# Splitting the last input projection of a forgetting-attention layer into a query half and a gate half, with the last four heads in one list of steps

## The chip, the cores and the metric

The kernel runs on one core of one Trainium2 chip. The metric is device time in microseconds (us) of one execution, from start to end, and the time of a kernel is the median of its runs. Engines are called by their names: TensorE (PE) for matrix products, with its weight load (PEld); VectorE (DVE) and ScalarE (ACT) for elementwise work; GpSimd (POOL); SyncE (SP), which here issues nearly all DMA transfers.

## The reference

Two layers over 512 tokens of width 2048. The first is differential attention; then keys, values and forget-gate logits are projected once (`shared_kv`); the second layer is forgetting attention, which the change touches:

```
def forgetting_attention(h, w_q, w_out, k, v, F):
    proj = h @ w_q
    q, g = jnp.split(proj, 2, axis=-1)
    q = q.reshape(B, S, B_HEADS, B_HEAD_DIM) * (B_HEAD_DIM ** -0.5)
    ...
        decay = jnp.moveaxis(Fq, 1, 2)[..., None] - Fk[:, :, None, :]
        sc = jnp.einsum('bqhd,bkhd->bhqk', qb, k).astype(f32) + decay
        sc = jnp.where(causal, sc, NEG)
        p = jax.nn.softmax(sc, axis=-1)
        return jnp.einsum('bhqk,bkhd->bqhd', p.astype(v.dtype), v)
    ...
    o = o.reshape(B, S, B_WIDTH) * jax.nn.silu(g)
    return o @ w_out
```

It has 16 heads of width 128. `q` is the left half of the projection's 4096 columns and the gate `g` the right half. The result goes through a residual sum and a layer norm.

## The kernel before, in words

**Numbers.** Every matrix operand is split into a high and a low part of a faster 32-bit format; a product is three matmuls (`products`, L172 to L176): high by high, high by low, low by high. A split is a copy on ScalarE and a subtraction on VectorE (`split`, L168 to L170). Tokens lie 128 to a block (4 blocks), the width in 16 row blocks of 128 (`KT`). `Hh[kt]`, `Hl[kt]` hold the transposed input of the running projection, 128 by 512; their 32 buffers turn in a ring (`new_h`).

**Weights.** All projections read one stream of weight tiles (`WeightStream`, L51). A `Job` names the columns, and one tile of it is two row blocks by 512 columns. SyncE loads a tile up to three ahead into four buffers (`wst`), ScalarE and VectorE split it two ahead into three buffers (`whi`, `wlo`, L94 and L95).

**Groups and ticks.** `group` (L303) runs a job: for each of 8 tiles, for each of 4 PSUM banks (`acc`), a burst of 6 matmuls. After each of the 32 bursts `tick` takes one piece from the list `pieces` and issues it, so the attention of an earlier pair of heads is laid between the bursts of a projection. `drain` issues all that is left. The program lists instructions in this order; when the kernel is built, a planner fixes each engine's order, and may put ready products ahead of ones that it expects to wait.

**The input projection of the second layer.** Eight jobs `bj[p]`, one for each pair of heads: 256 columns of queries and 256 of gates side by side. Banks 0 and 1 end as the queries of the two heads (`qh`, `ql`, L1201 and L1202), banks 2 and 3 as their gates (`sgb`, L1207 and L1208). While `bj[p]` runs, the pieces are the attention of pair p - 1 (`attention_pair`, L1303): 26 steps of `attention_b` (L1232). For each head and each of the four token blocks i:

- `score(i)`: products of queries and keys into one of two `sc` banks, then bias, sum and minimum, exponential, reciprocal and scaling (L1244 to L1255), on VectorE but for the exponential;
- `turn(i)`: a 32 by 32 transpose on VectorE (L1264) and a store to DRAM (L1266);
- `send(i)`: four DMAs from there into `pTl` (L1274);
- `take(i)`: the split of the transposed probabilities into `pTh` and `pTl` (L1280, L1281).

`values(0, 2)` and `values(2, 4)` then make the 12 matmuls of the head's output (bank `o`) and multiply by the gate into `ogB` (L1297). There is one `pTh` and one `pTl` for all heads. `load_pair` fetches a pair's values and decay rows, `split_pair` splits its values and keys (`vbh`, `kbh`); both are issued ahead of the last tile of the pair's own job.

**The end.** The outputs `ogB` of 16 heads, split by `split_ogb` (L1313) into new `Hh`, `Hl`, are the input of the output projection. While `bj[7]` runs, heads 0 to 13 are split, two after each tile from the second on. Queries of pair 7 are there only at the end of `bj[7]`, so its attention is laid between the bursts of the first output projection, with the split of heads 14 and 15 as the 27th step; row blocks 14 and 15 are read by the last of the 8 tiles. `out_projection` (L934) runs four jobs of 512 columns. Their residual work (`residual_b`, L1348) adds pieces `scaled` for each token block (`nr`, L1359 and L1360): for the first job into steps of `pieces` that are empty, from the third on, else at the end of the list. At the end of the first job it drains the list ahead of its first evacuation (`ztmp`, L961), and the attention's memory is given to the output.

Of the kernel before, what the change touches and what calls it, by code (L numbers as in the profile page):

```python
# [10 lines left out]
F32 = mybir.dt.float32  # L11
F32R = mybir.dt.float32r
# [4 lines left out]
P = 128  # L17
D = 2048
KT = D // P
# [15 lines left out]
class Job:  # L35


    def __init__(self, src, parts):
        self.src = src
        self.parts = parts  # L40
        self.width = sum(n for _, n in parts)

    def load(self, nc, dst, kt):
        rows = self.src[kt * P : (kt + 2) * P, :]
        off = 0
        for c, n in self.parts:
            nc.sync.dma_start(dst[:, :, off : off + n], rows[:, c : c + n].rearrange("(k p) n -> p k n", p=P))
            off += n


class WeightStream:  # L51
# [15 lines left out]
        self.order.append((job, sub))  # L67

    def add_job(self, job):
        for s in range(KT // 2):  # L70
            self.add(job, s)

    def load(self, upto):
# [37 lines left out]
def tile_yoco(  # L111
# [44 lines left out]
    def acc_bank(name="acc"):  # L156
        return ps.tile([P, 512], F32, name=name, tag="acc", bufs=4)
# [10 lines left out]
    def split(hi, lo, src):  # L168
        S.copy(hi, src)
        V.tensor_tensor(lo, src, hi.bitcast(F32), op=ALU.subtract)  # L170
# [96 lines left out]
    phases = [(0, 0, 4), (1, 0, 8), (0, 4, 12), (1, 8, 16), (0, 12, 16)]  # L267
    kj = [Job(kv_w, [(512 * g, 512)]) for g in range(4)]
    vj = [Job(kv_w, [(2048 + 512 * g, 512)]) for g in range(4)]
    bj = [Job(b_w_in, [(256 * p, 256), (2048 + 256 * p, 256)]) for p in range(8)]  # L270
    oA = [(f, Job(a_w_out, [(512 * f, 512)]), (0, 1, 2, 3)) for f in range(4)]
    oB = [(f, Job(b_w_out, [(512 * f, 512)]), (0, 1, 2, 3)) for f in range(4)]
    for u, k0, k1 in phases:
# [4 lines left out]
    for h in range(2, A_HEADS):  # L278
        ws.add_job(qk[h])
        ws.add_job(vg[h])  # L280
    for j in [o[1] for o in oA] + vj + kj + bj + [o[1] for o in oB]:
        ws.add_job(j)

    pieces = []
# [18 lines left out]
    def group(job, natural, evac, banks=range(4), bg=0, before_sub=None, after_sub=None, hold=0, after_held=None):  # L303


        acc = {b: acc_bank() for b in banks}
        w = job.width
        count = 0
        ns = KT // 2

        def burst(s, b, hi, lo):
            nonlocal count
            for kk in range(2):
                kt = 2 * s + kk
                bs = slice(b * P, (b + 1) * P)
                start, stop = kt == 0, kt == KT - 1
                if natural:
                    products(acc[b][:, :w], (Hh[kt][:, bs], Hl[kt][:, bs]), (hi[kk][:, :w], lo[kk][:, :w]), start, stop)
                else:
                    products(acc[b], (hi[kk][:, bs], lo[kk][:, bs]), (Hh[kt], Hl[kt]), start, stop)  # L320
            if s == ns - 1:
                evac(b, acc[b])
            tick(bg(count) if callable(bg) else bg)
            count += 1

        for s in range(ns - hold):
            if before_sub:
                before_sub(s)
            hi, lo = ws.get(job, s)
            for b in banks:  # L330
                burst(s, b, hi, lo)
            if after_sub:
                after_sub(s)
        for s in range(ns - hold + 3, ns):
            ws.advance(ws.where[(id(job), s)])

            pool, tag = (kpool, "K") if s < ns - hold + 5 else (hpool, "H")
            ws.step(lambda: pool.tile([P, 512], F32R, name="held", tag=tag))
            ws.load(ws.done + ws.STAGES - 1)
        held = [ws.get(job, s, 0) for s in range(ns - hold, ns)]  # L340
        for b in banks if hold else ():
            for k, (hi, lo) in enumerate(held):
                burst(ns - hold + k, b, hi, lo)
                if after_held:
                    after_held(b, k)
                if b == banks[-1] and k < 3:
                    ws.advance(ws.where[(id(job), ns - 1)] + 1 + min(k + 1, 3))


    def cols(name):  # L350
# [536 lines left out]
    for h in range(3, A_HEADS):  # L887
# [34 lines left out]
    def row_bcast(t, src):  # L922
        nc.sync.dma_start(t, src.partition_broadcast(P))
# [271 lines left out]
    def evac_b(p):  # L1195
        def fn(b, acc):
            hd = 2 * p + b % 2
            if b < 2:
                hi = bp.tile([P, T], F32R, name="qh", tag="qh", bufs=2)
                lo = bp.tile([P, T], F32R, name="ql", tag="ql", bufs=2)  # L1200
                S.activation(hi, acc, AF.Copy, scale=QS)  # L1201
# [10 lines left out]
    def load_pair(p):  # L1212
        v = bp.tile([P, TB, 256], F32, name="vld", tag="vld", bufs=1)
        nc.sync.dma_start(v, v_dram[:, 256 * p : 256 * (p + 1)].rearrange("(j p) e -> p j e", p=P))
        cur[p, "vld"] = v
        for hd in (2 * p, 2 * p + 1):
            nf = bp.tile([P, T], F32, name="nfb", tag="nfb", bufs=2)
            row_bcast(nf, f_dram[hd, :])
            cur[hd, "nf"] = nf

    def split_pair(p):
# [3 lines left out]
        cur[p, "vB"] = (vh, vl)  # L1225
        for hd in (2 * p, 2 * p + 1):
            kh = bp.tile([P, T], F32R, name="kbh", tag="kbh", bufs=2)
            kl = bp.tile([P, T], F32R, name="kbl", tag="kbl", bufs=2)
            split(kh, kl, KTs[hd])
            cur[hd, "kB"] = (kh, kl)  # L1230

    def attention_b(hd):  # L1232
        st = {}
# [79 lines left out]
    def split_ogb(hds):  # L1313
        for hd in hds:
            new_h(hd)
            split(Hh[hd], Hl[hd], ogB[hd])

    load_pair(0)
    for p in range(8):
# [110 lines left out]
```

## Time and profile before

| what | value |
|---|---|
| median of 3 runs | 1983.98 us (1981.49 to 1984.32) |
| span of the profiled execution | 1978.1 us |
| TensorE busy | 1936.2 us (98%), 8869 matmuls |
| VectorE busy | 1348.1 us (68%) |
| ScalarE busy | 704.0 us (36%) |
| mean granted clock of TensorE | 0.993 |
| mean DMA rate | 188 GB/s |

The profiled execution is given by its span, from its first to its last instruction; the time of a run also holds what lies around the span. A profile row names the line of the kernel, the engine, the operation and the tiles as `out<-in`. Times in rows are counted from the start of the span. "Idle before" is the time for which the engine stood still ahead of an instruction, with what released it. The granted clock is the share of full speed at which TensorE was allowed to run.

### The profile page before, as it was taken

What the parts mean: (1) busy time and instruction counts of PE and PEld (TensorE: products, weight loads), DVE (VectorE), ACT (ScalarE), POOL (GpSimd) and SP (SyncE); (2) the same over time, 40 slices, a digit from 0 to 9 for tenths busy, and PEclk for the clock granted to TensorE, in tenths of its full rate; (3) what the DMA queues carried; (4) which work ended last, traced back from release to release, by engine and by line L of the source; (5) the groups of instructions that cost most, each with busy time, mean ns of one, the idle gap of its engine ahead of it and who ended that gap; (6) DMA issues with size and microseconds to landing.
All of it is one profiled execution on the core that took longest, in us unless ns stands there. A gap on an engine that the chain in (4) does not pass through costs nothing.

```text
span 1978.1 us, 25283 instructions
## 1 busy us (share of the span) xinstructions
PE 1936.2 (98%) x8869; PEld 1600.8 (81%) x8869; DVE 1348.1 (68%) x2488; ACT 704.0 (36%) x1217; POOL 2.2 (0%) x10
## 2 busy tenths in 40 slices
PE   5999999999999999999999999999999999999997
PEld 4888888888887888788888888888888888887886
DVE  7885678777777778853575665666566666676657
ACT  2422445333332324431264222224343434453123
POOL 0000000000000000000000000000000000000000
PEclk8999999999999999999999999999999999999999
DMA  9993445676776777652345766664355555565522
GB/s 341 356 315 101 135 149 161 211 229 213 228 219 216 221 224 228 204 168 96 117 149 203 251 229 194 227 218 136 112 154 148 155 151 154 153 185 165 199 89 106
DMA packets 319515, 371.40 MB, mean 188 GB/s; under 512 B 57590, under 2 KB 221196, under 8 KB 318620
## 3 DMA queue, kind: packets, MB, share of 16 engines
q1 hardware_dynamic: 317008, 365.57, 58.2%
q10 hardware_dynamic: 2380, 4.21, 0.6%
q8 instruction: 70, 1.15, 0.2%
q14 instruction: 57, 0.47, 0.1%
HBM read 343.27 MB, written 26.43 MB: 187 GB/s over the span
## 4 chain that ended last, share of the span: by engine, by line
PE 87%; DVE 6%; DMA 4%; issue 1%; SPq 1%; ACT 1%; DVEq 0%; ACTq 0%
PE acc L174 25%; PE acc L175 25%; PE acc L176 25%; PE sc L175 2%; PE sc L176 2%; PE sc L174 2%; DMA ms<-in_kv_w_mod_dram 2%; PE o L174 1%; PE o L176 1%; PE o L175 1%; DVE macc L391 1%; DVE wlo L95 1%; DMA sms<-in_w_mod_dram 1%; DMA e<-turned 1%; DMA turned<-e 1%
## 5 line engine op out<-in xcount | busy, mean ns | idle before, releaser
L95 DVE TENSOR_TENSOR wlo<-wst,whi 128x1024 fp32r<-128x1024 f32 (+2 forms) x322 | 384.3, 1195 | 352.3 <-ACT whi L94 349.3
L94 ACT CAST whi<-wst 128x1024 fp32r<-128x1024 f32 (+2 forms) x322 | 331.8, 1031 | 724.9 <-PE acc L176 355.6
L174 PE MATMUL acc<-whi,hh 128*128 128x512 f32 x1232 | 483.3, 395 | 4.1 <-DVE sg L695 2.2
L175 PE MATMUL acc<-wlo,hh 128*128 128x512 f32 x1232 | 482.1, 391 | 0.1
L176 PE MATMUL acc<-whi,hl 128*128 128x512 f32 x1232 | 481.4, 391 | 0.0
L174 PE MATMUL acc<-hh,whi 128*128 128x512 f32 x1184 | 464.2, 392 | 1.7 <-DVE sg L695 1.6
L175 PE MATMUL acc<-hl,whi 128*128 128x512 f32 x1184 | 461.5, 390 | 0.0
L176 PE MATMUL acc<-hh,wlo 128*128 128x512 f32 x1184 | 460.7, 390 | 0.0
L174 PEld LDWEIGHTS acc<-whi,hh 128*128 128x128 f32 x1232 | 232.6, 189 | 51.3 <-issue 2.6
L176 PEld LDWEIGHTS acc<-whi,hl 128*128 128x128 f32 x1232 | 232.2, 188 | 49.1
L175 PEld LDWEIGHTS acc<-wlo,hh 128*128 128x128 f32 x1232 | 232.5, 189 | 46.2 <-DVE wlo L95 0.5
L176 PEld LDWEIGHTS acc<-hh,wlo 128*128 128x128 f32 x1184 | 222.3, 188 | 47.6
L174 PEld LDWEIGHTS acc<-hh,whi 128*128 128x128 f32 x1184 | 222.5, 188 | 46.2 <-issue 2.5
L175 PEld LDWEIGHTS acc<-hl,whi 128*128 128x128 f32 x1184 | 222.6, 188 | 42.0
L391 DVE SCALAR_TENSOR_TENSOR macc<-ms,cact,macc 128x512 f32<-128x512 f32 x300 | 223.7, 746 | 34.2 <-DMA ms<-in_kv_w_mod_dram 17.5
L498 DVE SCALAR_TENSOR_TENSOR sacc<-sms,cact,sacc 128x512 f32<-128x512 f32 (+1 forms) x127 | 89.5, 705 | 5.1 <-DMA sms<-in_w_mod_dram 1.4
L725 ACT ACTIVATE e<-e,mn 128x128 f32<-128x128 f32 (+3 forms) x64 | 36.0, 563 | 111.6 <-DVE mn L721 107.3
L1253 ACT ACTIVATE eb<-eb,mnb 128x128 f32<-128x128 f32 (+1 forms) x64 | 36.0, 563 | 85.9 <-DVE mnb L1250 85.7
L721 DVE CUSTOM_DVE_ANT_0 e<-sc,bias 128x128 f32<-128x128 f32 (+3 forms) x64 | 31.1, 486 | 22.0 <-PE sc L176 21.9
L391 DVE SCALAR_TENSOR_TENSOR macc<-msk,cact,macc 128x512 f32<-128x512 f32 x60 | 45.0, 750 | 1.4
L1250 DVE CUSTOM_DVE_ANT_0 eb<-sc,biasb 128x128 f32<-128x128 f32 (+1 forms) x64 | 31.1, 485 | 19.5 <-PE sc L176 18.8
L822 ACT ACTIVATE ogT<-tr,subg 128x128 f32<-128x128 f32 x64 | 20.0, 364 | 46.0 <-PE tr L820 45.9
(262 smaller groups left out, 1764.5 us busy)
## 6 DMA issues: line engine op xcount, KB each, us to landing
wst<-in_a_w_in_dram SPq DMA_DIRECT2D x240, 256.0 KB, 3.9
ms<-in_w_mod_dram SPq DMA_DIRECT2D x64, 512.0 KB, 4.2
ms<-in_kv_w_mod_dram SPq DMA_DIRECT2D x64, 512.0 KB, 4.3
wst<-in_kv_w_dram SPq DMA_DIRECT2D x64, 512.0 KB, 3.8
wst<-in_b_w_in_dram SPq DMA_DIRECT2D x128, 256.0 KB, 3.0
sms<-in_w_mod_dram SPq DMA_DIRECT2D x56, 512.0 KB, 6.9
wst<-in_a_w_out_dram SPq DMA_DIRECT2D x32, 512.0 KB, 3.7
msk<-in_w_mod_dram SPq DMA_DIRECT2D x64, 256.0 KB, 5.3
```

Source lines behind the costliest of these rows:

```text
L94: self.nc.scalar.copy(hi[:, :, :w], st[:, :, :w])
L95: self.nc.vector.tensor_tensor(lo[:, :, :w], st[:, :, :w], hi[:, :, :w].bitcast(F32), op=ALU.subtract)
L174: PE.matmul(dst, lhs[0], rhs[0], start=start, stop=False)
L175: PE.matmul(dst, lhs[0], rhs[1], start=False, stop=False)
L176: PE.matmul(dst, lhs[1], rhs[0], start=False, stop=stop)
L391: ins = V.scalar_tensor_tensor(acc, w, cact[:, kt : kt + 1], acc, op0=ALU.mult, op1=ALU.add)
L498: V.scalar_tensor_tensor(acc, w, sc, acc, op0=ALU.mult, op1=ALU.add)
L721: V.tensor_tensor_reduce(out=e[:, :w], in0=sc[:, :w], in1=st["bias"][:, (3 - i) * P :], scale=-1.0, scalar=3.0e38, op0=ALU.add, op1=ALU.mi ...
L725: S.activation(e[:, :w], e[:, :w], AF.Exp, bias=mn, scale=-1.0, accum_out=rs)
L822: S.activation(ogT[2 * h + e][:, i * P : (i + 1) * P], pt[:, e * P : (e + 1) * P], AF.Copy, scale=subg[:, e : e + 1])
L1250: V.tensor_tensor_reduce(out=e[:, :w], in0=sc[:, :w], in1=bias[:, :w], scale=-1.0, scalar=3.0e38, op0=ALU.add, op1=ALU.min, accum_out=mn)
L1253: S.activation(e[:, :w], e[:, :w], AF.Exp, bias=mn, scale=-1.0, accum_out=rs)
```

## The change

`bj` keeps seven jobs. The eighth becomes two half jobs: `lastq`, the 256 query columns of heads 14 and 15, and `lastg`, their 256 gate columns. A tile of a half job is four row blocks by 256 columns. `half_group` runs it in two banks with 16 bursts of 6 matmuls. In `lastg` the outputs of heads 0 to 7 are split, one after every second burst. The attention of pairs 6 and 7 becomes one list of 50 steps, `last_pairs`, that starts with `lastq` and runs on into the first output projection; in it heads 14 and 15 follow behind 12 and 13, and the loads and splits of their decay rows, keys and values and the splits of heads 8 to 15 are steps of their own. The lines that laid the attention of pair 7 into the output projection go.

```
+class HalfJob:
+    def __init__(self, src, col):
+        self.src, self.col = src, col
+        self.width = 512
+        self.subs = KT // 4
+    def load(self, nc, dst, kt):
+        rows = self.src[2 * kt * P : (2 * kt + 4) * P, self.col : self.col + 256]
+        nc.sync.dma_start(dst.rearrange("p k (q n) -> p k q n", q=2), rows.rearrange("(k q p) n -> p k q n", q=2, p=P))
...
-    bj = [Job(b_w_in, [(256 * p, 256), (2048 + 256 * p, 256)]) for p in range(8)]
+    bj = [Job(b_w_in, [(256 * p, 256), (2048 + 256 * p, 256)]) for p in range(7)]
+    lastq, lastg = HalfJob(b_w_in, 256 * 7), HalfJob(b_w_in, 2048 + 256 * 7)
...
+    def half_group(job, evac, after_sub):
+        acc = [acc_bank() for _ in range(2)]
+        for s in range(job.subs):
+            hi, lo = ws.get(job, s)
+            for k in range(2):
+                for b in range(2):
+                    for q in range(2):
+                        kt = 4 * s + 2 * k + q
+                        bs = slice(256 * q + b * P, 256 * q + (b + 1) * P)
+                        products(acc[b], (hi[k][:, bs], lo[k][:, bs]), (Hh[kt], Hl[kt]), kt == 0, kt == KT - 1)
+                    if kt == KT - 1:
+                        evac(b, acc[b])
+                    tick(0)
+                after_sub(2 * s + k)
...
+    def last_pairs():
+        sa, ra, da, ta, va = attention_b(12)
+        sb, rb, db, tb, vb = attention_b(13)
+        sc, rc, dc, tc_, vc = attention_b(14)
+        sd, rd, dd, td, vd = attention_b(15)
+        kc, kd = (partial(split_k, hd) for hd in (14, 15))
+        fc, fd = (partial(load_f, hd) for hd in (14, 15))
+        lv, v7 = partial(load_v, 7), partial(split_v, 7)
+        og = [lambda hd=hd: split_ogb((hd,)) for hd in range(B_HEADS)]
+        steps = [
+            [], [sa[0]], [sa[1], lv], [ra[0]], [sa[2], ra[1]], [da[0]], [sa[3], da[1]], [ra[2], fc],
+            [sb[0], ta[0]], [ra[3], da[2]], [sb[1], ta[1]], [rb[0], da[3]], [sb[2], ta[2]], [rb[1]], [sb[3], ta[3]], [rb[2], va[0], fd],
+            [va[1], kc], [db[0], db[1], rb[3]], [db[2], sc[0]], [tb[0], db[3]], [sc[1], tb[1]], [tb[2], kd], [sc[2], tb[3]], [vb[0]],
+            [vb[1], rc[0]], [sc[3], rc[1]], [dc[0], dc[1], v7], [rc[2]], [sd[0]], [tc_[0], rc[3], dc[2]], [tc_[1], dc[3]], [sd[1]],
+            [tc_[2]], [sd[2], tc_[3], og[8]], [rd[0], vc[0]], [vc[1], rd[1]], [sd[3], og[9]], [dd[0], dd[1], rd[2]], [og[10]],
+            [rd[3], dd[2]], [dd[3], og[11]], [td[0]], [td[1], og[12]], [td[2]], [td[3], og[13]], [vd[0]], [vd[1]], [], [og[14]], [og[15]],
+        ]
+        return [todo or None for todo in steps]
...
-        def after(s):
-            if s >= 1:
-                split_ogb((2 * s - 2, 2 * s - 1))
...
-        group(bj[p], False, evac_b(p), before_sub=before, after_sub=after if p == 7 else None)
+        group(bj[p], False, evac_b(p), before_sub=before)
+
+    pieces.extend(last_pairs())
+    half_group(lastq, evac_b(7), lambda s: None)
+    half_group(lastg, lambda b, acc: evac_b(7)(b + 2, acc), lambda s: split_ogb((s,)))
...
-    pieces.extend(attention_pair(7))
-    pieces.append(lambda: split_ogb((14, 15)))
```

Here `s`, `r`, `d`, `t` and `v` with a letter a to d for heads 12 to 15 are `score`, `turn`, `send`, `take` and `values`; `kc`, `kd` split a key, `fc`, `fd` load decay rows, `lv` and `v7` load and split the values of pair 7, and `og` splits a head's output. `load_pair` and `split_pair` are cut into `load_v`, `load_f`, `split_v` and `split_k`, with the same operations.

More of the change, by code (lines that the diff above doesn't have):

```diff
@@ L41, in __init__ @@
         self.width = sum(n for _, n in parts)
+        self.subs = KT // 2
     def load(self, nc, dst, kt):
@@ L69, in add_job @@
     def add_job(self, job):
-        for s in range(KT // 2):
+        for s in range(job.subs):
             self.add(job, s)
@@ L280, in tile_yoco @@
         ws.add_job(vg[h])
-    for j in [o[1] for o in oA] + vj + kj + bj + [o[1] for o in oB]:
+    for j in [o[1] for o in oA] + vj + kj + bj + [lastq, lastg] + [o[1] for o in oB]:
         ws.add_job(j)
@@ L347, in group @@
                     ws.advance(ws.where[(id(job), ns - 1)] + 1 + min(k + 1, 3))
+    def half_group(job, evac, after_sub):
+        acc = [acc_bank() for _ in range(2)]
+        for s in range(job.subs):
+            hi, lo = ws.get(job, s)
[9 more added lines that the diff above has]
+                after_sub(2 * s + k)
     def cols(name):
@@ L1210, in evac_b, with load_v @@
         return fn
-    def load_pair(p):
+    def load_v(p):
         v = bp.tile([P, TB, 256], F32, name="vld", tag="vld", bufs=1)
@@ L1215, in load_pair, with load_f, split_v @@
         cur[p, "vld"] = v
+    def load_f(hd):
+        nf = bp.tile([P, T], F32, name="nfb", tag="nfb", bufs=2)
+        row_bcast(nf, f_dram[hd, :])
+        cur[hd, "nf"] = nf
+    def load_pair(p):
+        load_v(p)
         for hd in (2 * p, 2 * p + 1):
[L1217 to L1221, printed above, removed]
+            load_f(hd)
+    def split_v(p):
         vh = bp.tile([P, TB, 256], F32R, name="vbh", tag="vbh", bufs=1)
@@ L1225, in split_pair, with split_k @@
         cur[p, "vB"] = (vh, vl)
+    def split_k(hd):
+        kh = bp.tile([P, T], F32R, name="kbh", tag="kbh", bufs=2)
+        kl = bp.tile([P, T], F32R, name="kbl", tag="kbl", bufs=2)
+        split(kh, kl, KTs[hd])
+        cur[hd, "kB"] = (kh, kl)
+    def split_pair(p):
+        split_v(p)
         for hd in (2 * p, 2 * p + 1):
[L1227 to L1230, printed above, removed]
+            split_k(hd)
     def attention_b(hd):
@@ L1316, in split_ogb @@
             split(Hh[hd], Hl[hd], ogB[hd])
+    def last_pairs():
[16 more added lines that the diff above has]
+        return [todo or None for todo in steps]
     load_pair(0)
-    for p in range(8):
+    for p in range(7):
         if p:
```

## The prediction

> **What bounds the kernel now.** I read the page first, then the busy time by stage around the place that the change touches, then the waits of TensorE, then the instructions of TensorE and VectorE in order of time.
>
> ```profile
> span 1978.1 us, 25283 instructions
> ...
> PE 1936.2 (98%) x8869; PEld 1600.8 (81%) x8869; DVE 1348.1 (68%) x2488; ACT 704.0 (36%) x1217; POOL 2.2 (0%) x10
> ```
>
> The page says that TensorE is the bound, busy for 1936.2 of 1978.1 us. The change removes no product, so it can only win back idle or slow time of TensorE. Where is that? The stages, in order: the last input projection (job `bj[7]`, which carries the attention of pair 6), the first output projection up to its seventh weight tile, its end, and the start of the second. Columns: length, busy time per engine, granted clock, DMA share.
>
> ```profile
> core 0: us, PE busy (x) PEld busy (x) DVE busy (x) ACT busy (x) POOL busy (x), PEclk, DMA share, GB/s
> 1722.70:1776.90 54.20, 54.20 (x253) 45.26 (x252) 43.39 (x89) 29.78 (x56) 0.00 (x0) 1.00 0.58 172
> ...
> 1776.90:1820.80 43.90, 43.90 (x205) 36.82 (x204) 28.85 (x67) 15.76 (x32) 0.00 (x0) 1.00 0.52 154
> 1820.80:1834.60 13.80, 9.87 (x28) 7.64 (x27) 10.52 (x18) 1.38 (x2) 0.00 (x0) 0.63 0.91 319
> 1834.60:1845.00 10.40, 9.92 (x44) 7.83 (x44) 10.28 (x17) 1.34 (x2) 0.00 (x0) 1.00 0.42 159
> ```
>
> The first two stages are full at full clock. The third is not: 28 matmuls in 13.8 us, and the granted clock fell to 0.63. The waits of TensorE from 1480 us to the end name the causes; there are only three (us in total, times, longest).
>
> ```profile
> PE o L175 <- DVE pTl L1281: 2.5, 1, 2.5
> PE acc L174 <- ACT hh L169: 1.4, 1, 1.4
> PE acc L174 <- DVE ztmp L961: 0.5, 1, 0.5
> ```
>
> TensorE in order of time, start and length first. A busy span has a modelled end, so I count from start to start.
>
> ```profile
> 1804.81 0.40 PE L175 MATMUL o<-pTl,vbh 128*128 128x512 f32 x1
> ...
> 1806.54 0.39 PE L174 MATMUL acc<-whi,hh 128*128 128x512 f32 x1
> ...
> 1820.60 0.39 PE L176 MATMUL acc<-whi,hl 128*128 128x512 f32 x1
> 1820.83 0.40 PE L174 MATMUL o<-pTh,vbh 128*128 128x512 f32 x1
> 1823.72 0.51 PE L175 MATMUL o<-pTl,vbh 128*128 128x512 f32 x1 [2.50 <-DVE pTl L1281]
> ...
> 1826.41 0.41 PE L176 MATMUL o<-pTh,vbl 128*128 128x256 f32 x1
> 1828.25 0.80 PE L174 MATMUL acc<-whi,hh 128*128 128x512 f32 x1 [1.43 <-ACT hh L169]
> ...
> 1834.39 0.41 PE L176 MATMUL acc<-whi,hl 128*128 128x512 f32 x1
> 1834.65 0.39 PE L174 MATMUL acc<-whi,hh 128*128 128x512 f32 x1
> ...
> 1839.45 0.61 PE L174 MATMUL acc<-whi,hh 128*128 128x512 f32 x2
> 1840.54 0.50 PE L174 MATMUL acc<-whi,hh 128*128 128x512 f32 x1 [0.48 <-DVE ztmp L961]
> ```
>
> From 1806.54 to 1820.60 there are 62 steps of a wide product: 0.2268 us each. The last eleven value products of a head took 1806.54 - 1804.81 = 1.73 us at full clock. At 1820.83 TensorE has done all of the first output projection that doesn't need heads 14 and 15, starts the values of head 15 (`o`), and waits for that head's probabilities (`pTl`), then for its gated output as `hh`. What held `pTl` back stands on VectorE and ScalarE:
>
> ```profile
> 1819.32 1.03 ACT L1280 CAST pTh<-pTl 128x384 fp32r<-128x384 f32 x2
> ...
> 1820.59 0.55 DVE L1281 TENSOR_TENSOR pTl<-pTl,pTh 128x384 fp32r<-128x384 f32 x1
> 1821.05 0.68 DVE L1359 SCALAR_TENSOR_TENSOR nr<-nr,g 128x512 f32<-128x512 f32 x1
> ...
> 1822.98 0.68 DVE L1281 TENSOR_TENSOR pTl<-pTl,pTh 128x512 fp32r<-128x512 f32 x1
> ...
> 1828.23 0.69 DVE L170 TENSOR_TENSOR hl<-ogB,hh 128x512 fp32r<-128x512 f32 x1 [0.68 <-ACT hh L169]
> ...
> 1839.80 1.28 DVE L961 TENSOR_TENSOR ztmp<-acc,gate 128x512 f32<-128x512 f32 x2
> ```
>
> ScalarE had its half by 1820.35; VectorE ran residual pieces (`nr`) in between. More such pieces, run by the drain at burst 28, delay the evacuation `ztmp` to 1839.80.
>
> **What the end of attention costs now.** From 1820.60 to 1834.65 are 14.05 us. The wide acc products in it number 16 (one before, 15 from 1828.25 to 1834.39): 16 x 0.2268 = 3.63; the twelve value products 0.23 + 1.73 = 1.96. Work 5.59, loss 8.46 us: the wait of 1823.72 - 1820.83 - 0.23 = 2.66, the gap 1828.25 - 1826.41 - 0.21 = 1.63 (0.21 is a 256-wide step at that clock), and 4.17 that the low clock costs. The second wait: 1840.54 - 1839.45 = 1.09 for two products of 0.45, so 0.64. **Together 9.1 us, all there is to win.**
>
> **Part by part.** *The projection in halves.* Old: 8 weight tiles of two row blocks by 512 columns, 4 banks of 6 products per tile. New: 4 + 4 tiles of four row blocks by 256 columns, 2 banks of 6 products, twice per tile. So 192 products of 0.2268 us on both sides, 24 per tile, and as many weight splits on ScalarE and VectorE: no change. SyncE issues 8 loads of 512 KB in place of 16 of 256 KB, with the same 1 KB rows. Such a load isn't in the trace; the nearest one is
>
> ```profile
> wst<-in_kv_w_dram SPq DMA_DIRECT2D x64, 512.0 KB, 3.8
> ```
>
> The stream loads three tiles ahead, 3 x 24 x 0.2268 = 16.3 us at the least, so a landing of twice 3.8 us is hidden. Bounds: 0 (hidden) and 3.8 (one tile late); I take 0, since no row shows TensorE waiting for a weight load. Fewer issues could only free SyncE, which doesn't set the end; a gain is excluded.
>
> *Queries first.* Their two evacuations now come half a job earlier. In the old order head 14's first score could only follow these at the end of the job:
>
> ```profile
> 1752.88 0.40 PE L174 MATMUL o<-pTh,vbh 128*128 128x512 f32 x1
> ...
> 1771.39 0.40 PE L174 MATMUL o<-pTh,vbh 128*128 128x512 f32 x1
> ...
> 1769.55 0.60 ACT L1201 ACTIVATE qh<-acc 128x512 fp32r<-128x512 f32 x1 [0.76 <-PE acc L176]
> ```
>
> The first two rows are the values of heads 12 and 13, 18.5 us apart. One pair of probability tiles (`pTh`, `pTl`) serves all heads, so heads go through it one after the other, and this is the length of one turn. The values of 14 had to wait until 1804.12, for the scores came after 1769.55.
>
> *The list of steps.* There are 50 steps for 32 bursts of the two half jobs, so 18 are left for the first output projection, the split of head 15 being its 18th. With turns of 18.5 us head 15's values start at 1752.88 + 3 x 18.5 = 1808.4 (the list starts one burst earlier, which I don't count). Then 1.96 for the products and three operations of 0.69 at most: ready by 1812.4. TensorE needs it when all else is done, 1820.83 as now plus the twelve value products that then lie ahead: 1822.8. **Slack 10.4 us.** So 2.66 + 1.63 + 4.17 go. What is late next is nothing in this projection. Four residual pieces fill a free step and the three behind, and the pieces of the second block, drained today at burst 28, get ticks of their own before it; so the 0.64 goes too.
>
> *Queues moved past.* The splits of heads 8 to 13, today in the projection, move behind it: six pairs of casts on ScalarE and VectorE leave the fullest stretch. In their place come scores of 14 and 15. The key and value splits and the loads of decay rows are spread as single steps, each behind the last use of the buffer it takes. SyncE issues in order, and already waits on VectorE:
>
> ```profile
> SPq L1266 <- DVE tb L1264: 20.1, 9, 4.8
> ```
>
> This (us in total, times, longest) is the longest entry between 1720 and 1840 us; sends to the next head and weight loads queue behind it, under 4.8 us at a time, covered by the 16.3 us above.
>
> *VectorE in the gate half.* The price list is from the groups between 1722.7 and 1776.9 us (columns: busy, mean ns):
>
> ```profile
> L95 DVE TENSOR_TENSOR wlo<-wst,whi 128x1024 fp32r<-128x1024 f32 x9 | 11.0, 1221 | 0.9 <-ACT whi L94 0.9
> L170 DVE TENSOR_TENSOR hl<-ogB,hh 128x512 fp32r<-128x512 f32 x13 | 8.8, 674 | 3.6 <-PE acc L175 3.6
> L1244 DVE SCALAR_TENSOR_TENSOR biasb<-nfb,F,mask 128x128 f32<-128x128 f32 (+3 forms) x8 | 4.3, 540 | 0.0
> L1264 DVE STREAM_TRANSPOSE tb<-eb 128x128 f32<-128x128 f32 (+3 forms) x8 | 4.1, 508 | 0.1
> L1281 DVE TENSOR_TENSOR pTl<-pTl,pTh 128x128 fp32r<-128x128 f32 (+3 forms) x8 | 3.9, 482 | 1.3 <-ACT pTh L1280 1.3
> L1250 DVE CUSTOM_DVE_ANT_0 eb<-sc,biasb 128x128 f32<-128x128 f32 (+3 forms) x8 | 3.8, 477 | 0.9 <-PE sc L176 0.8
> L1255 DVE TENSOR_SCALAR eb<-eb,rsb 128x128 f32<-128x128 f32 (+3 forms) x8 | 3.1, 383 | 0.1
> ```
>
> Steps 16 to 31 hold six scores (0.540 + 0.477 + 0.383 = 1.40 each: 8.4), five transposes (2.5), six takes (2.9), eight head splits (5.4), four weight splits (4.9), and some nine other operations (two evacuations of queries, two gated outputs, two key splits, one value split of 1.2, two reciprocals) at about 0.65: 5.9. Sum 30. TensorE's work there is 96 x 0.2268 = 21.8, one and a half heads of values 2.9, and for the 18 products of the scores an estimated 18 x 0.157 = 2.8 (1.73 / 11, the mean step of the value products): 27.5 us. Consecutive VectorE operations overlap (the take at 1820.59 lasts 0.55, the next starts after 0.46), which takes about a tenth off: 27 against 27.5. VectorE is just full there, so it may run a few us late; the weight splits are taken two tiles ahead (48 x 0.2268 = 10.9 us), and the lag is worked off in the output projection. I allow 0.2 us per head in four heads where a value product catches VectorE late: **0.8 us**, between 0 and, each, the 2.66 above; the nearer end is 0, because at full load about 1753 us no wait is listed.
>
> **Sum.** 1978.1 - 9.1 + 0.8 = 1969.8 us of span. The median of 1983.98 is 5.9 us more than the profiled span; with the same around it, **1975.7 us**, 0.42% less. A measurement of this kernel can tell about 0.2%, 4 us, from no change.
>
> **Rivals.** *One stall comes back.* The order of instructions on each engine is fixed when the kernel is built; if VectorE runs late against it at one `o`, TensorE waits once as at 1820.83 and drops its clock again: 2.66 + 4.17 = 6.8 of the 9.1 given back, 1981.7 us. For it: VectorE just full over 27 us. Against: it was nearly full in the first half of `bj[7]` too, and no wait is listed there:
>
> ```profile
> 1722.70:1749.00 26.30, 26.30 (x124) 22.05 (x123) 24.77 (x61) 15.30 (x33) 0.00 (x0) 1.00 0.56 168
> ```
>
> VectorE was busy for 24.77 of 26.30 us there. The clock's part is read from the stage with 0.63, after an idle span of 2.50 us, while the one of 0.48 left it at 1.00.
>
> [...]
>
> *It doesn't do what it says.* Head 15 still comes last, because the one probability tile and SyncE's order stretch each of three turns by (10.4 + 2.7) / 3 = 4.4 us; the wait then stands where it is: 1984.
>
> *Slower.* VectorE decides: the scores and transposes of a head (4 x 1.40 + 4 x 0.508 = 7.6 us) don't fit beside the turn of the head before but lengthen it. This decides from 5.9 us a turn, where head 15 is 7.3 us late. With two turns lengthened by 7.6 and eight more head splits (5.4) in the way it is (15.2 + 5.4) - 10.4 = 10.2 us late; with the gap and the clock (1.63 + 4.17) the end costs 16.0 in place of 9.1: 1991. For it: the single buffer and the full gate half. Against: the turn from 1752.88 to 1771.39 lies in a stage in which VectorE is idle for 10.8 us (43.39 busy of 54.20).
>
> **Numbers.** The forecast has 0.70, one stall back 0.13, nothing changed 0.07, slower 0.10. The forecast's own spread goes from the fastest earlier run less all the gain, 1981.49 - 9.1 = 1972.4, to one wait of 2.66 without the clock, 1978.4. Taking in the first rival the range is 1972.0 to 1982.0; the other two, 0.17, lie outside. Faster by over 0.2% (below 1980.0): the forecast and part of the first rival, 0.75; within: 0.15; slower (above 1988): 0.10.
>
> **What would show it.** Right: no `PE o <- DVE pTl` of 2.5, no clock below 1.00 between 1720 us and the end of the projections, `hl` of head 15 ending over 5 us ahead of the first product that reads it, `ztmp` no longer listed, span near 1970. Wrong: a granted clock under 1.00 in the two half jobs, value products of heads 13 to 15 more than 22 us apart, waits for `wlo` or `wst` on TensorE, or TensorE idle at the seventh tile of the first output projection.

## The result and the profile after

The changed kernel took 1979.66 us (median of 20 runs, 1975.28 to 1984.45), the kernel before 1982.70 us on the same chip (20 runs, 1980.62 to 1985.63). The ratio is 0.9983, 95% interval 0.9977 to 0.9989: faster by some 0.17%, where 0.42% was forecast. The interval doesn't reach 1, so that is a gain, but a smaller one than the 0.2% named in the prediction. The profiled execution took 1978.08 us, 1.8 of it around the span.

First the stages of the changed kernel, cut at the same places of its work (columns as in the prediction). The rows are the two halves of the stage that carries the attention of pairs 6 and 7, two stretches of the first output projection, the change to the second, and the first products of that.

```profile
span 1976.3 us, 25268 instructions
```

```profile
core 0: us, PE busy (x) PEld busy (x) DVE busy (x) ACT busy (x) POOL busy (x), PEclk, DMA share, GB/s
1722.70:1749.00 26.30, 26.30 (x124) 22.03 (x123) 23.75 (x59) 12.49 (x27) 0.00 (x0) 1.00 0.52 159
1749.00:1776.90 27.90, 27.90 (x135) 23.34 (x134) 27.10 (x61) 18.77 (x38) 0.00 (x0) 1.00 0.51 148
1776.90:1805.00 28.10, 28.10 (x131) 23.56 (x130) 17.14 (x34) 10.71 (x20) 0.00 (x0) 1.00 0.69 209
1805.00:1826.40 21.40, 21.40 (x99) 17.65 (x97) 12.65 (x20) 4.72 (x6) 0.00 (x0) 1.00 0.78 278
1826.40:1836.80 10.40, 6.17 (x18) 4.84 (x18) 10.40 (x19) 1.04 (x1) 0.00 (x0) 0.67 0.45 169
1836.80:1845.00 8.20, 8.20 (x38) 6.76 (x37) 2.81 (x3) 1.99 (x2) 0.00 (x0) 1.00 0.53 175
```

TensorE is full at full clock to 1826.4, through the place where it stood still before. The loss has moved behind it: 18 matmuls in 10.40 us at a clock of 0.67, with VectorE busy for all 10.40. The waits of TensorE from 1480 us on have one entry left, in place of three:

```profile
PE acc L188 <- DVE ztmp L994: 4.2, 1, 4.2
```

`ztmp` is the copy that takes a finished sum out of its bank at the end of the first output projection. The second projection needs that bank. TensorE around the wait, with the first product that reads head 15's split (`hl`) on top:

```profile
1822.04 0.39 PE L190 MATMUL acc<-whi,hl 128*128 128x512 f32 x1
...
1826.12 0.39 PE L190 MATMUL acc<-whi,hl 128*128 128x512 f32 x1
1830.74 0.79 PE L188 MATMUL acc<-whi,hh 128*128 128x512 f32 x1 [4.23 <-DVE ztmp L994]
...
1835.47 0.40 PE L190 MATMUL acc<-whi,hl 128*128 128x512 f32 x1
1835.70 0.39 PE L188 MATMUL acc<-whi,hh 128*128 128x512 f32 x1
```

The stall is 1830.74 - 1826.12 - 0.23 = 4.39 us. The twelve products from 1830.74 to 1835.70 take 4.96 us where 12 x 0.2268 = 2.72 would do: 2.24 for the clock. Together 6.6 of the 9.1 us have come back. What VectorE did in that time:

```profile
1818.83 0.69 DVE L1342 SCALAR_TENSOR_TENSOR ogB<-o,sgb 128x512 f32<-128x512 f32 x1 [2.83 <-PE o L190]
1819.43 0.68 DVE L1425 SCALAR_TENSOR_TENSOR nr<-nr,g 128x512 f32<-128x512 f32 x1
1820.15 0.69 DVE L1426 SCALAR_TENSOR_TENSOR nr<-b,nr 128x512 f32<-128x512 f32 x1
1820.76 0.69 DVE L184 TENSOR_TENSOR hl<-ogB,hh 128x512 fp32r<-128x512 f32 x1
1821.36 0.68 DVE L1425 SCALAR_TENSOR_TENSOR nr<-nr,g 128x512 f32<-128x512 f32 x1
1822.24 1.23 DVE L109 TENSOR_TENSOR wlo<-wst,whi 128x1024 fp32r<-128x1024 f32 x1 [0.19 <-ACT whi L108]
...
1828.80 1.28 DVE L1426 SCALAR_TENSOR_TENSOR nr<-b,nr 128x512 f32<-128x512 f32 x2
1830.00 1.28 DVE L994 TENSOR_TENSOR ztmp<-acc,gate 128x512 f32<-128x512 f32 x2
```

From the gated output of head 15 to the first `ztmp` VectorE has one row of work with a single gap of 0.19 us. In it are 14 residual operations (`nr`), 0.60 us from start to start: 8.4 of 11.2 us. They belong to two output blocks: those of the first block that stand behind head 15 in the list, and all of the second block's, for which there is no hurry.

The time of an execution also moves for reasons that lie far ahead of the change: in the traces below head 11's values start anywhere from 1718.85 to 1726.04 us. So the traces are compared below by one distance that leaves those out: from the first value product of head 11 to the last matmul of the kernel. What the clock does within that stretch is still in it (R1 to R4 below). It is 1965.50 - 1718.85 = 246.65 us before and 1963.70 - 1719.68 = 244.02 us after, 2.6 us less.

### The profile page after: what moved, and what is told of

Read it like the earlier page. It is cut to its first block, busy times and chain, and to the rows that moved or that the text cites. A ratio compares the mean times of both kernels' runs of the same rounds, so it can differ in the third digit from the quotient of the medians.

```text
span 1976.3 us, 25268 instructions
## 1 busy us (share of the span) xinstructions
PE 1934.1 (98%) x8869; PEld 1599.5 (81%) x8869; DVE 1346.3 (68%) x2488; ACT 703.2 (36%) x1217; POOL 2.2 (0%) x10
## 4 chain that ended last, share of the span: by engine, by line
PE 88%; DVE 7%; DMA 3%; issue 1%; SPq 1%; ACT 1%; DVEq 0%; ACTq 0%
PE acc L188 26%; PE acc L189 26%; PE acc L190 25%; PE sc L188 2%; PE sc L189 2%; PE sc L190 2%; PE o L188 1%; DVE macc L424 1%; PE o L190 1%; PE o L189 1%; DMA ms<-in_kv_w_mod_dram 1%; DVE wlo L109 1%; DVE sacc L531 1%; DMA sms<-in_w_mod_dram 1%; DMA turned<-e 0%
## 5 line engine op out<-in xcount | busy, mean ns | idle before, releaser
L424 DVE SCALAR_TENSOR_TENSOR macc<-ms,cact,macc 128x512 f32<-128x512 f32 x300 | 223.5, 745 | 34.4 <-DMA ms<-in_kv_w_mod_dram 18.6
```

The costliest lines, as they stand in the source:

```text
L424: ins = V.scalar_tensor_tensor(acc, w, cact[:, kt : kt + 1], acc, op0=ALU.mult, op1=ALU.add)
```

## The experiments

**Theory.** What is left of the stall is VectorE's order: residual operations stand ahead of the first copy of the sums. They stand there because head 15's steps come late in the list and the residual pieces lie among or behind them. The main rival is that head 15 is itself too late, or the half jobs cost something, so that the order of the residual work doesn't matter.

**E1: second block's residual late.** In the changed kernel, the residual of the second output block is prepared only after the first evacuation.

```diff
-                pieces.extend([None] * (8 if k else 0) + [lambda k=k: prepare(k + 1)])
+                if k:
+                    pieces.extend([None] * 8 + [lambda k=k: prepare(k + 1)])
...
                 if f == 0 and b == 0:
                     drain()
                     opened()
+                    if layer == 1:
+                        pieces.extend([None] * 3 + [lambda: prepare(1)])
```

> The changed kernel, but the residual pieces of the second output block are made only after the first evacuation of the first block, so that they run in the second projection. Theory A (the wait of 4.2 us for ztmp is VectorE working off residual pieces ahead of the evacuations): 8 of the 14 such operations leave, 8 x 0.6 = 4.8 us, so ztmp starts about 4.8 us earlier, the wait falls to under 0.5 us, the clock stays at 1.00 there, and the span falls by the 4.4 of the stall and the 2.4 of the clock, from 1976.3 to about 1969.5 us; time 0.35% under the changed kernel. Theory B (head 15 is late, so the last products and with them every evacuation are late, whatever VectorE does in between): the wait stays at 3 to 4 us, time unchanged within 0.1%.

Measured: 1974.18 us against 1983.80 of the kernel before on the chip that E1, E3, E4 and E5 shared, ratio 0.9948 (0.9935 to 0.9960). No wait over 0.2 us is left on TensorE. VectorE in this run, with the first copy (`ztmp`) at 1828.18 and five residual operations ahead of it, not 14; and below it TensorE's stages:

```profile
1822.42 0.69 DVE L1345 SCALAR_TENSOR_TENSOR ogB<-o,sgb 128x512 f32<-128x512 f32 x1 [2.83 <-PE o L190]
...
1827.58 0.69 DVE L1428 SCALAR_TENSOR_TENSOR nr<-nr,g 128x512 f32<-128x512 f32 x1
1828.18 0.68 DVE L997 TENSOR_TENSOR ztmp<-acc,gate 128x512 f32<-128x512 f32 x1
```

```profile
1722.70:1820.00 97.30, 97.30 (x455) 81.31 (x454) 75.33 (x160) 46.35 (x89) 0.00 (x0) 1.00 0.55 165
1820.00:1845.00 25.00, 25.00 (x115) 20.87 (x114) 21.61 (x32) 4.84 (x5) 0.00 (x0) 1.00 0.79 275
```

From the gated output to the first copy are 5.8 us, not 11.2, and TensorE is full at full clock throughout (second fence). The distance is 237.55 us: 246.65 - 237.55 = 9.10, the whole loss that the prediction had worked out.

**E3: first block's residual early.** In the changed kernel, the four residual pieces of the first block are hung on the 6th to 9th step that then stand in the list, not on free steps or its end.

```diff
-            free = [k for k, piece in enumerate(pieces) if piece is None and k > 1]
-            for k, b in zip(free, banks):
-                pieces[k] = lambda b=b: scaled(b)
-            pieces.extend(lambda b=b: scaled(b) for b in banks[len(free):])
+            for k, b in zip(range(5, 9), banks):
+                todo = pieces[k] if isinstance(pieces[k], list) else [pieces[k]] if pieces[k] else []
+                pieces[k] = [*todo, lambda b=b: scaled(b)]
```

> The changed kernel, but the four residual pieces of the first output block are hung on the 6th to 9th step of the first output projection instead of behind the last value step. Theory A: the pieces of the first block (6 of the 14 operations ahead of ztmp, 3.6 us) are done before head 15 arrives, the wait of 4.2 us falls to under 1 us, the span to about 1970 us. Theory B: wait of 3 to 4 us as it is, time unchanged within 0.1%.

Measured: 1973.82 us, ratio 0.9950 (0.9938 to 0.9962), distance 237.79 us, no wait over 0.3 us. Fewer operations ahead of the copy do as well as later ones: the theory's second way to the same place. In this trace none of the 14 is left between the gated output (1820.80) and the first copy (1825.36): the eight of the second block, which the edit doesn't move, now run behind it. So it took away more than the six expected.

**E5: takes ahead of the weight split.** The values of heads 12 to 15 start at 1751.30, 1769.92, 1790.20 and 1816.20 us in the changed kernel: turns of 18.6, 20.3 and 26.0 us, where the prediction had 18.5 throughout. The last two of these starts, and ScalarE in between:

```profile
1790.20 0.40 PE L188 MATMUL o<-pTh,vbh 128*128 128x512 f32 x1
...
1816.20 0.40 PE L188 MATMUL o<-pTh,vbh 128*128 128x512 f32 x1
```

```profile
1797.41 1.05 ACT L108 CAST whi<-wst 128x1024 fp32r<-128x1024 f32 x1 [3.24 <-PE acc L190]
1798.37 0.29 ACT L1325 CAST pTh<-pTl 128x128 fp32r<-128x128 f32 x1
1802.85 1.05 ACT L108 CAST whi<-wst 128x1024 fp32r<-128x1024 f32 x1 [4.19 <-issue]
1803.81 0.40 ACT L1325 CAST pTh<-pTl 128x256 fp32r<-128x256 f32 x1
1808.29 1.05 ACT L108 CAST whi<-wst 128x1024 fp32r<-128x1024 f32 x1 [4.08 <-issue]
1809.25 1.02 ACT L1325 CAST pTh<-pTl 128x384 fp32r<-128x384 f32 x2
```

Each take of head 15 (`pTh`) comes right behind a weight split (`whi`) ahead of which ScalarE stood still for 3 to 4 us. E5 keeps the weight splits of the first output projection in the order in which the program lists them, so that the planner can't put them ahead of the takes.

```diff
...
-            self.nc.scalar.copy(hi[:, :, :w], st[:, :, :w])
+            ins = self.nc.scalar.copy(hi[:, :, :w], st[:, :, :w])
+            if job in self.pinned:
+                self.pin(ins)
...
+    ws.pin, ws.pinned = tc.keep_in_program_order, (oB[0][1],)
     out_projection(oB, 1, zp2, open_z, residual_b, norm_b)
```

> The changed kernel, but the weight splits of the first output projection are pinned on ScalarE in the order of the program, so that the takes of head 15 no longer stand behind splits that wait for TensorE. If that queue is what made the last turn 26 us long: the takes follow their landings at 1794 to 1802 us, head 15's value products move from 1816.2 to about 1806 to 1810 us, the residual pieces of the first block follow them, and the wait for ztmp goes: span about 1969.5 to 1971 us. If the turn is as long for another reason (landings, SyncE): value products stay near 1816 and the time unchanged within 0.1%.

Measured: 1973.56 us, ratio 0.9952 (0.9941 to 0.9964), distance 237.68 us. ScalarE in this run, and the start of head 15's values:

```profile
1796.47 0.30 ACT L1328 CAST pTh<-pTl 128x128 fp32r<-128x128 f32 x1 [0.46 <-DMA pTl<-turned]
1798.30 0.41 ACT L1328 CAST pTh<-pTl 128x256 fp32r<-128x256 f32 x1 [1.53 <-DMA pTl<-turned]
1803.65 0.51 ACT L1328 CAST pTh<-pTl 128x384 fp32r<-128x384 f32 x1 [4.94 <-DMA pTl<-turned]
1804.07 1.99 ACT L109 CAST whi<-wst 128x1024 fp32r<-128x1024 f32 x2
1805.96 0.62 ACT L1328 CAST pTh<-pTl 128x512 fp32r<-128x512 f32 x1
```

```profile
1811.03 0.40 PE L191 MATMUL o<-pTh,vbh 128*128 128x512 f32 x1
```

Three of the four takes now wait for their own data (`<-DMA`); the fourth comes right behind two weight splits, with no idle time ahead of it. The last turn is 1811.03 - 1792.05 = 19.0 us, and TensorE no longer waits for the copy, although residual operations still stand ahead of it. So the 7 us by which the last turn was too long come from ScalarE's queue, and the stall needs both: a late head 15 and the residual work behind it. One of the two may stay.

**E4: half jobs with the old lists.** The kernel before with `lastq` and `lastg`, but with the attention of pairs 6 and 7 in two separate lists as before.

```diff
-    pieces.extend(last_pairs())
+    pieces.extend(attention_pair(6)[1:])
...
     half_group(lastq, evac_b(7), lambda s: None)
-    half_group(lastg, lambda b, acc: evac_b(7)(b + 2, acc), lambda s: split_ogb((s,)))
+    half_group(lastg, lambda b, acc: evac_b(7)(b + 2, acc), after_gates)
...
+    pieces.extend(attention_pair(7))
+    pieces.append(lambda: split_ogb((14, 15)))
```

(Against the changed kernel; `after_gates` splits two earlier heads after each unit from the second on, and after the sixth drains the list and loads and splits pair 7.)

> The changed kernel with its two half jobs, but the lists of steps as they were: attention of pair 6 in the half jobs (one empty step fewer), that of pair 7 in the first output projection. My theory (only the list moves time; the half jobs cost and give nothing): the waits of the kernel before come back, 2.5 us for pTl and 1.4 us for hh with the clock down, time as before, 1982 to 1984 us. Rival (the halves themselves give the gain, by queries being there earlier): 1979 to 1980 us.

Measured: 1980.91 us, ratio 0.9985 (0.9976 to 0.9993), distance 245.21 us. All three old waits are there, in other sizes:

```profile
PE acc L188 <- DVE ztmp L994: 2.3, 1, 2.3
PE acc L188 <- ACT hh L183: 1.4, 1, 1.4
PE o L189 <- DVE pTl L1326: 1.4, 1, 1.4
```

The half jobs alone don't remove the waits. That it came out under the kernel before was a miss, and its 0.9985 can't be told from the 0.9983 of the whole change: the rival, that the halves themselves give what the change gained, had 1979 to 1980 us and isn't ruled out by the times. The distance, from one trace, is 1.2 to 1.5 us longer than in the two traces of the changed kernel. The shorter wait for `pTl` is the visible difference from before; what made it shorter wasn't tried.

**E2: kernel before, second block's residual late.** The edit of E1, made in the kernel before.

> The kernel before (its old lists of steps, whole projections), with only the late preparation of the second block's residual. Theory A (the projected lists are what frees the end, and VectorE's order alone isn't enough): the residual operations that belong to the first block still stand ahead of the last copy of values that TensorE waits for, so only the second wait of 0.64 us goes; the time is 0 to 0.1% below the kernel before, some 1983 us. Rival (VectorE's order was the whole trouble from the start): the 2.5 us wait and the low clock go as well, and the time falls by 0.4 to 0.5%, to some 1975.

Measured: 1979.15 us, ratio 0.9981 (0.9971 to 0.9991), against 1983.12 us of the kernel before on this chip: more than the theory allowed, less than the rival. The waits are those of before without `ztmp`, and one of 0.2 for a weight split. The distance is 243.38 us, 3.3 less, with only 0.64 of it in the wait that went. The rest is the clock, low for a shorter time behind the same wait of 2.5 us: 3.4 us, not 10.0, by the reckoning under R1 to R4. The ratio is that of the whole change (0.9983), from an edit of a few lines. The runs R1 to R4 follow this up.

**E8: kernel before with both residual edits.** The edits of E1 and E3 in the kernel before.

> The kernel before with both moves of the residual operations: the first block's among the steps of head 15, the second block's late. None of them stands ahead of the last copy of values any more. Theory A: the wait for that copy shrinks from 2.5 to under 0.8 us, the gap of some 1.6 us for want of other work stays; if the clock then holds, the loss at the end of attention falls from 9.1 to some 2.3 us and the time to some 1977 (0.35% down); if it still drops, 0.1 to 0.15% down. It ends above the changed kernel with the same moves in each case. Rival (the lists are worth nothing of their own): as fast as the changed kernel with the moves, 0.5% down, 1974.

Measured: 1975.72 us, ratio 0.9965 (0.9953 to 0.9978), distance 239.29 us. One wait is left, and the clock holds:

```profile
PE acc L174 <- ACT hh L169: 1.4, 1, 1.4
...
1820.00:1845.00 25.00, 23.52 (x106) 19.19 (x105) 18.69 (x27) 4.58 (x7) 0.00 (x0) 1.00 0.81 279
```

So 246.65 - 239.29 = 7.4 of the 9.1 us could be had without the change, by the order of VectorE's work alone; the medians give the same 7.4 (1983.12 - 1975.72). The wait that is left, from the values of head 15 to its split output, needs other work beside it, and that is what the overlapped list provides: 239.29 - 237.69 = 1.6 us, by the distance of E6 below, which has the same edits and the change. The times don't show this 1.6: E6 took 1975.27 us on the same chip, within the noise of E8.

**E6: changed kernel with both residual edits.**

> The changed kernel with both moves of the residual operations. Theory A: either of them alone already took the whole wait and the low clock away, so there is nothing left for the two together: ratio 0.995 to the kernel before, some 1974 us, last value product to last product as with one of them. Rival (each takes away a part of its own): 0.993 or less, 1970.

Measured: 1975.27 us, ratio 0.9962 (0.9950 to 0.9975), distance 237.69 us. By the distance there is nothing more to win than with one of them, as expected. E1, E3, E5 and E6 lie within 0.24 us of each other by distance, and their intervals overlap. Each beats the kernel before on its own chip, and each interval lies below that of the changed kernel (0.9977 to 0.9989), which has a single run on these chips (R4, 1984.13 us). The spans of E1, E3 and E5, 1973.4, 1972.0 and 1971.8 us, are 0.8 to 3.9 above the expected ones; in these traces head 11's values already start 1.8 to 3.6 us later than in the first trace of the changed kernel.

**R1 to R4: how long the clock stays low.** Both kernels and E2, unchanged, traced again.

> The kernel before, unchanged, for another trace of it. Theory C (how long the clock stays low after one wait is a draw of the single execution, in steps of some 3.4 us): the same wait of 2.5 us for the last copy of probabilities, but a low clock of 3.4 or 6.8 us in at least one of the traces of this kernel, where the first had 10.2; from the values of head 11 to the last product 243 to 247 us. Rival D (the length belongs to the order of instructions): 10.2 us again and 246.6.

> The same as the run before it, once more: theory C, a length of 3.4 or 6.8 us is seen among these traces; rival D, 10.2 us in each.

> The kernel before with the late preparation of the second block's residual, once more. Its first trace had the same wait of 2.5 us, but a low clock of only 3.4 us, and 243.4 us from the values of head 11 to the last product. Theory C: 3.4, 6.8 or 10.2 us, 243 to 247 us, not the same for certain. Rival D: 3.4 us again and 243.4.

> The changed kernel, unchanged, for another trace of it. Its wait of 4.2 us for the first copy of the sums stands in the order of the instructions and comes back in each theory. Theory C: the low clock behind it, 6.8 us in the first trace, may be 3.4 or 10.2 here, and the 244.0 us from the values of head 11 to the last product move by some 1.7 with it. Rival D: 6.8 us and 244.0 again.

The waits of TensorE over 0.3 us in R1 and then in R2, the same program as the kernel before:

```profile
PE o L175 <- DVE pTl L1281: 2.5, 1, 2.5
PE acc L174 <- DVE ztmp L961: 1.8, 1, 1.8
PE acc L174 <- ACT hh L169: 1.4, 1, 1.4
```

```profile
PE o L175 <- DVE pTl L1281: 2.5, 1, 2.5
PE acc L174 <- DVE ztmp L961: 2.3, 1, 2.3
PE acc L174 <- ACT hh L169: 1.4, 1, 1.4
```

The wait for `pTl` is 2.5 us in all three traces of this program. The 10.2 us behind it, from 1824.00 to 1834.20, first in the trace of the prediction, then in R1, then in R2:

```profile
1824.00:1834.20 10.20, 8.77 (x25) 7.06 (x25) 6.96 (x12) 0.98 (x2) 0.00 (x0) 0.51 1.01 354
```

```profile
1824.00:1834.20 10.20, 8.02 (x27) 6.64 (x28) 7.22 (x13) 1.15 (x2) 0.00 (x0) 0.67 0.99 348
```

```profile
1824.00:1834.20 10.20, 7.26 (x34) 6.06 (x35) 9.12 (x16) 1.67 (x2) 0.00 (x0) 1.00 1.03 335
```

At the low clock a wide product takes a step of 0.43 us (1832.18 to 1832.61 in the changed kernel's first trace), not 0.2268, and the granted clock is 0.50 (1830 to 1834 us there). If low means 0.50 throughout, a stretch was low for 2 x (1 - granted clock) x its length, an estimate: 10.0 us in the first trace, nearly all of it, 6.7 in R1, and not at all in R2. In the same way E2 was low for 3.4 us and R3, the same program, for 6.9 (0.79 and 0.57 from 1826 to 1834); the changed kernel for 6.9 in its first trace (0.57 from 1828 to 1836) and 3.4 in R4 (0.79 from 1834 to 1842). So the length differs between executions of one program, as theory C says and rival D doesn't.

Two distances missed, though. R4's moved by 0.3 us, not 1.7: of the first trace's 6.9 us at the low clock some 2.3 lie in the wait itself (0.59 from 1828.00 to 1830.74), where TensorE has nothing to lose, of R4's 3.4 some 0.2. And R1's, 248.06, lies above the 243 to 247 expected, where the wait for `ztmp` was 1.8 us, not 0.5, and behind it the clock fell a second time, for 3.4 us:

```profile
1840.00:1848.00 8.00, 6.70 (x22) 5.38 (x23) 6.54 (x10) 1.05 (x1) 0.00 (x0) 0.79 0.23 69
```

R2 also shows what a held clock is worth here: TensorE reaches the end of the projection earlier and waits there instead (2.3 us for `ztmp`, not 0.5), because VectorE isn't done. The distances:

| run | program | from, us | to, us | distance |
|---|---|---|---|---|
| trace of the prediction | before | 1718.85 | 1965.50 | 246.65 |
| R1 | before | 1719.89 | 1967.95 | 248.06 |
| R2 | before | 1720.63 | 1965.32 | 244.69 |
| E2 | before, late | 1723.44 | 1966.82 | 243.38 |
| R3 | before, late | 1721.65 | 1965.58 | 243.93 |
| first trace | changed | 1719.68 | 1963.70 | 244.02 |
| R4 | changed | 1726.04 | 1969.74 | 243.70 |
| E8 | before, both | 1719.60 | 1958.89 | 239.29 |
| E1 | changed, late | 1723.24 | 1960.79 | 237.55 |

The means are 246.5 for the kernel before, 243.7 for E2 and 243.9 for the changed kernel. So E2's gain is some 2.8 by distance, in which the second wait, 0.5 to 2.3 us, counts more than the one trace of before had shown. These are two or three traces each, and those of the kernel before spread over 3.4 us. R4 has the wait of 4.2 us again.

## Why the prediction was right in places and wrong in the sum

**What could be won: right.** The 9.1 us were the loss of that execution, to the tenth (E1). But the 4.17 us in it for the clock were one draw: the kernel before lies 248.06 - 237.55 = 10.5 above the best distance in R1 and 244.69 - 237.55 = 7.1 in R2.

**The old waits go: right.** No `o <- pTl` and no `hh` is listed, and the clock is 1.00 until 1826.4.

**The halves and the full gate half: right.** In this trace TensorE waits for no weight tile. VectorE was forecast at 27 us of 27.5 in the gate half and shows 27.10 of 27.90, without a wait of TensorE; the 0.8 us that I allowed there weren't needed.

**Turns of 18.5 us: a step that failed.** "With turns of 18.5 us head 15's values start at ... 1808.4" carried one turn of an earlier stage over to all three. They start at 1816.20, 7.8 us later. I had named the queues that steps are moved past, but of ScalarE's I had counted only the casts that leave it, and not that a weight split that waits there holds up the takes behind it (E5: 7.0 of these us). The turn of 20.3 us wasn't followed up. Head 15's split (`hl`) ends at 1820.76 + 0.69 = 1821.45, some 0.6 us ahead of the first product that reads it, at 1822.04 where the first bank of the last tile ends. The slack of 10.4 us was nearly all used, and just enough.

**"What is late next is nothing in this projection ... so the 0.64 goes too": the step that cost the time.** I worked out the slack of `hl` and not that of the copy behind it, and counted ticks of the list, not time of VectorE. From the start of head 15's values to its gated output are 1818.83 - 1816.20 = 2.63 us, from there to the first copy 11.17, and 0.74 more until TensorE has its bank. If that row of work keeps its length, it ends at 1822.9 from the forecast start of 1808.4, and TensorE is through at 1826.12 + 0.23 = 1826.35: by this estimate the copy had a slack of 3.4 us, not of 10.4. Head 15 came 7.8 us late, and 7.8 - 3.4 = 4.4 is the stall. The 3.4 is at the upper end: in E5, with head 15 early, the row from its gated output (1813.42) to the copy (1827.32) was 13.9 us long, not 11.2, as more weight splits and one more residual operation ran in it. So either repair is enough: head 15 on time (E5), or fewer residual operations ahead of the copy (E1, E3).

**The rivals.** "One stall comes back" is what happened in kind and size (6.6 us, where it had 6.8), but at another place and by another mechanism: not VectorE late in the gate half, but work queued ahead of the copy that frees the banks. The granted clock fell with the wait of 4.2 us in both traces of the changed kernel (0.57 over 8 us in the first, 0.79 in R4), and behind the wait of 2.5 us in two of the three traces of the kernel before (0.51 and 0.67 over 10.2 us, 1.00 in R2). "It doesn't do what it says" came in part: the three turns grew by 0.1 + 1.8 + 7.5 = 9.4 us of the 13.1 that it needed, most of it by ScalarE's queue, which it didn't name; the old wait didn't come back. "Slower" didn't occur.

**The signs.** Of the five signs of being right only the first came, no `o <- pTl`. The clock fell below 1.00, `hl` ended 0.6 us ahead and not 5, `ztmp` is listed, and the span isn't near 1970. One sign of being wrong came: values of two heads more than 22 us apart (26.0).

**The time.** The span was forecast at 1969.8 us and is 1976.3, 6.5 off. The time was forecast at 1975.7 and is 1979.66, 4.0 off. The difference is the 5.9 us that I put around the span: only 1.8 lie around it, the rest was the distance of a quick profiled execution from the median of its runs (1.6 us in the changed kernel). That the time lies inside the range owes something to luck: the forecast's own spread ended at 1978.4, and the room above it was there for a stall by another mechanism. A change within 0.2% had a chance of 0.15.

## What to carry to other kernels

When a stall at the end of a stage is removed, work out the slack of the thing that TensorE needs *after* it too, from all that each engine has queued ahead of that, in microseconds and not in steps of a list. Work without a due date that sits in front of a copy which frees a bank is the first to move: here two edits of a few lines to VectorE's order, without the change, gave 7.4 of 9.1 us (E8). When steps of a chain are moved, look at every queue that they cross, the elementwise engine's with its waiting casts too, before a turn measured elsewhere is reused.

## What the runs showed of the hardware that I had not expected

Behind the same wait of 2.50 us the granted clock stayed at 1.00 (R2), or fell to half for some 6.7 us (R1) and for 10.0 (the first trace). Behind R1's wait of 1.8 us it fell too, for 3.4 us (0.79 from 1840 to 1848); behind the wait of 1.4 us that E8 has left it didn't (1.00 from 1820 to 1845). So no length of the wait tells here whether the clock falls: it fell behind 1.8 us and held behind 2.50.

A low clock also falls far ahead of this work: E1 has two such stretches (columns as above), each behind a wait of TensorE for `sg`, a tile of the first layer:

```profile
524.79 0.47 PE L188 MATMUL acc<-hh,whi 128*128 128x512 f32 x1 [1.90 <-DVE sg L728]
820.72 0.47 PE L188 MATMUL acc<-whi,hh 128*128 128x512 f32 x1 [2.12 <-DVE sg L728]
```

```profile
524.00:528.00 4.00, 3.21 (x8) 2.56 (x9) 3.33 (x7) 3.03 (x8) 0.00 (x0) 0.64 0.56 151
820.00:828.00 8.00, 7.28 (x28) 6.03 (x29) 6.49 (x16) 3.39 (x10) 0.00 (x0) 0.79 0.71 218
```

Low for 2 x (1 - 0.64) x 4.00 = 2.9 us in the first and 2 x (1 - 0.79) x 8.00 = 3.4 us in the second, and so half of that lost. In the first trace of the kernel before TensorE waits 2.17 us for the same tile, up to 817.80, longer than either, and the clock stays at 1.00 (810 to 834). Such draws may be part of why runs of one kernel spread over 5 us and more: the slowest run of the changed kernel, 1984.45 us, has a mean clock of 0.991, its other runs 0.993 to 0.995. They are also a reason to compare these versions by a distance inside the trace beside the medians.
